# A float32 encoder trunk on one core: hidden tiles of two feed-forwards by seven block products in place of eight

## The chip, the core and the metric

The kernel runs on one core of one Trainium2 chip. The core's engines work side by side: TensorE (PE; its weight loads appear as PEld) multiplies into PSUM, which here is eight banks of 128x512 float32. VectorE (DVE), ScalarE (ACT) and GpSimd (POOL) work element by element, and SyncE (SP) issues most DMAs. Each engine runs its instructions in order. The metric is device time in microseconds from launch to end; lower is better.

## The reference, cut to what matters

One layer over 1024 prompt and 32 sample tokens, with D = 1024 features, 2816 hidden features and a modulation of nine rows computed from a condition vector c. All is float32.

```python
def swiglu(h, w1, w3, w2):
    return (jax.nn.silu(h @ w1) * (h @ w3)) @ w2

mod = (silu(c) @ w_ada + b_ada).reshape(B, 9, D)      # per group: prompt, sample
modulate(h, k) = h * (1 + mod[3k+1]) + mod[3k];  gate(k) = 1 + mod[3k+2]

x = layer_norm(x)
x = layer_norm(ALPHA*x + 0.5*gate(0) * swiglu(modulate(x, 0), ffn1_w1, ffn1_w3, ffn1_w2))
x = layer_norm(ALPHA*x + gate(1) * mixing(modulate(x, 1)))    # recurrent and gated branch
x = layer_norm(ALPHA*x + 0.5*gate(2) * swiglu(modulate(x, 2), ffn2_w1, ffn2_w3, ffn2_w2))
```

## The kernel before

**Layout.** Activations lie feature-major: features on the 128 partitions, eight feature tiles k, tokens along the free axis in three chunks of 384, 384 and 288 (the last ends with the 32 sample tokens). Products keep float32 precision by parts: each operand is split into a high part and a low part (type float32r), and a product is three passes over TensorE, high by high, high by low, low by high. `xh` and `xl` are the two parts of the modulated x, one tile for each chunk; `whl` holds the two parts of a weight tile. A split is a ScalarE copy (L177) for the high part and a subtraction (L178) on VectorE for the low part; while a norm follows a feed-forward, GpSimd does the subtraction.

**Feed-forward.** There are 22 hidden tiles of 128 features. `H(nf, t)` makes one: for w1, then w3, eight k-steps times three chunks times three passes, 144 matmuls, all through L132. ScalarE takes silu from PSUM (L659), VectorE multiplies by the w3 product (L666), and a split gives the two parts of `g`, the hidden tile. `F(nf, block)` multiplies the block's hidden tiles by w2 for eight output feature tiles m and three chunks; VectorE's `add_gated` (L713) multiplies each result by its gate and adds it into `xacc` (in the profile xa, and xb in the second feed-forward). A block is two hidden tiles, the last two blocks are [18] and [19, 20, 21]; F of a block comes one hidden tile after the block is complete.

**Weights.** 156 tiles of 128x1024 stream in the order of use: SP loads one into `raw` (four buffers), it is split into `whl` (five buffers), and `w_rel` goes on when a product has been issued.

**Beside the first feed-forward** `ada_rest` makes modulation rows 2 to 8, each in two halves of 512. VectorE adds up weight times condition in `acc` (L603), 16 instructions a half; TensorE sums over the partitions (psm); ScalarE copies the row out; GpSimd's queue issues a DMA to DRAM (`mrow`, L622) and two back (`mod`, L625). Such side programs are Python generators: `go` starts one and `poll`, called at each product, lets it write its next instructions when TensorE's program has advanced by as many us as it yielded. So the order on TensorE is that of the program; a scheduler orders the other engines' instructions.

Then come a layer norm, mixing, another norm, the second feed-forward with the same functions, and the last norm. The inner loop and the release of weights are

```python
for q in range(2):                                   # w1, w3
    w = self.w_get((f"f{nf}w{(1, 3)[q]}", t))
    ps = [self.ps() for _ in range(3)]
    for k in range(K):
        for c in range(3):
            self.h_mm(ps[c], w, c, k, k == 0, k == K - 1)
    self.w_rel()
```

Of the kernel before, what the change touches and what calls it, by code (L numbers as in the profile page):

```python
# [12 lines left out]
F32 = mybir.dt.float32  # L13
# [16 lines left out]
# token chunks; the last one ends with the 32 sample tokens  # L30
# [4 lines left out]
# columns of the packed per-feature vectors  # L35
# [37 lines left out]
def ffn_order():  # L73
    """Program of one feed-forward: ('H', t) and ('F', block), in order."""
    o = [("H", 0), ("H", 1)]
    nxt = 2
    for b in BLOCKS[:-1]:
        o.append(("H", nxt))
        nxt += 1
        o.append(("F", b))  # L80
        if len(b) == 2 and nxt < 19:
            o.append(("H", nxt))
            nxt += 1
    while nxt < FF:
        o.append(("H", nxt))
        nxt += 1
    o.append(("F", BLOCKS[-1]))
    return o


def stream_order():
    s = []
    for n in (1, 2):
        for kind, a in ffn_order():
            if kind == "H":
                s += [(f"f{n}w1", a), (f"f{n}w3", a)]
# [12 lines left out]

class Core:  # L110
    def __init__(self, tc, ins, outs):
        self.tc, self.nc = tc, tc.nc
        self.i, self.o = ins, outs
        self.pe = 0.0
        self.side = []
        self.ntot = 2
        self.mods = set()
        self.window = False
        self.ln_out = {}

# [14 lines left out]
    def go(self, gen, kind=None):  # L135
        """Run a side program beside the main one; it yields the time it has to wait."""
# [15 lines left out]
    def drain(self, e, out=False):  # L152
        """Finish a side program, or a norm up to its output; earlier norms first."""
# [7 lines left out]
    def w_init(self):  # L161
        self.order = stream_order()
        self.raws = {}
        self.ws = {}
        self.n_raw = self.n_split = self.n_rel = self.n_get = 0

    def w_raw(self):
        n = self.n_raw
        if n >= len(self.order):
            return  # L170
        r = self.wpool.tile([P, 1024], F32, tag="raw", name="raw", bufs=4)
        self.nc.sync.dma_start(r, self.i["wst"][n])
        self.raws[n] = r
# [5 lines left out]

    def w_split(self, e=None):  # L180
# [28 lines left out]
    def run(self):  # L209
# [4 lines left out]
        # pools over PSUM have eight one-bank buffers  # L214
# [38 lines left out]
        with tc.manual_schedule(engines={E.DVE, E.Activation, E.Pool}):  # L253
# [38 lines left out]
    def startup(self):  # L292
# [29 lines left out]
        # silu(c) in its two parts: [feature, k, (part, group)]  # L322
# [1028 lines left out]
```

## Time and profile before

| | us |
|---|---|
| median of three runs | 1987.72 |
| lowest and highest | 1986.25, 1989.53 |
| span of the profiled execution, first to last instruction | 1981.3 |
| the median less that span | 6.4 |
| TensorE busy | 1931.3 (97%) |
| VectorE busy | 1096.0 (55%) |
| ScalarE busy | 540.8 (27%) |
| GpSimd busy | 90.4 (5%) |

The span is the profiled execution's own time; what lies around it (launch and end) is in the runs alone. Busy shares are means over stages: start to 137 us, first feed-forward to 820 (the modulation's side program runs to 640), norm and mixing to 1211, second feed-forward to 1920, last norm to 1982. In a row of a timeline the first number is the start in us, the second the duration; "x12" counts instructions merged into the row, and square brackets give the idle time of that engine ahead of it and what ended it.

### The profile page before, as it was taken

The page shows a single profiled execution, that of the slowest core. Times are in us where ns is not written, and L with a number is a line of the kernel's source. Part 1 is how long each engine was busy: PE and PEld are TensorE (multiplying, and loading weights), DVE is VectorE, ACT ScalarE, POOL GpSimd, SP SyncE. Part 2 cuts the span into 40 slices and gives each one's busy share as a digit, 9 for nine tenths or more (in the row PEclk, how much of TensorE's full clock was granted, in tenths as well). Part 3 has the DMA queues.
Part 4 walks back from the last instruction along what each step waited for, and adds up shares of the span by engine and source line. Part 5 has one row for each costly group of instructions (what it writes and reads, how often), then busy time and mean ns, then how long its engine had stood idle before and what let it go on. Part 6 is the DMA issues. An engine that isn't in the chain of part 4 may idle for free.

```text
span 1981.3 us, 27961 instructions
## 1 busy us (share of the span) xinstructions
PE 1931.3 (97%) x11818; PEld 1886.5 (95%) x11818; DVE 1096.0 (55%) x1988; ACT 540.8 (27%) x848; POOL 90.4 (5%) x102
## 2 busy tenths in 40 slices
PE   7999999999999999989999999999999999999996
PEld 4899999999999999989889999999999999999996
DVE  8885765765664344763977375432442343244457
ACT  6542121212112111244544347111111111111114
POOL 2100000000000000022000000000000000000000
PEclk9999999999999999989899999999999999999998
DMA  7333223222322111121012311111111111110102
GB/s 281 130 126 101 95 84 117 97 75 96 102 95 71 54 43 44 54 80 67 14 59 67 130 36 40 54 43 54 43 34 63 43 43 44 54 43 33 33 1 88
DMA packets 40429, 140.13 MB, mean 71 GB/s; under 512 B 5588, under 2 KB 8276, under 8 KB 39536
## 3 DMA queue, kind: packets, MB, share of 16 engines
q1 hardware_dynamic: 37040, 128.98, 18.8%
q10 hardware_dynamic: 1920, 9.24, 1.2%
q0 software_dynamic: 1344, 0.12, 0.4%
q8 instruction: 93, 1.52, 0.3%
q14 instruction: 32, 0.26, 0.0%
HBM read 129.53 MB, written 8.79 MB: 70 GB/s over the span
## 4 chain that ended last, share of the span: by engine, by line
PE 78%; issue 10%; DVE 7%; ACT 2%; DMA 2%; POOL 0%; SPq 0%; POOLq 0%; DVEq 0%; ACTq 0%
PE ps L132 74%; PE psl L132 1%; DVE xl L462 1%; DVE acc L603 1%; PE psm L132 1%; PE psa L132 1%; DMA mod<-mrow 1%; PE psg L132 1%; DVE tot L719 0%; DMA mrow<-row 0%; ACT t L452 0%; DMA raw<-ada 0%; DVE xa L713 0%; DVE xb L832 0%; DVE t L843 0%
## 5 line engine op out<-in xcount | busy, mean ns | idle before, releaser
L132 PE MATMUL ps<-xh,whl 128*128 128x384 f32 (+1 forms) x5184 | 1245.4, 324 | 2.4 <-ACT xh L459 1.9
L132 PEld LDWEIGHTS ps<-xh,whl 128*128 128x128 f32 x5184 | 910.5, 189 | 7.0 <-ACT xh L459 2.1
L132 PE MATMUL ps<-xl,whl 128*128 128x384 f32 (+1 forms) x2592 | 839.3, 324 | 4.2 <-DVE xl L462 4.2
L132 PE MATMUL ps<-g,whl 128*128 128x384 f32 (+1 forms) x3168 | 522.2, 325 | 1.8 <-DVE xa L713 1.3
L132 PEld LDWEIGHTS ps<-g,whl 128*128 128x128 f32 x3168 | 513.2, 189 | 6.8 <-DVE xa L713 1.9
L132 PEld LDWEIGHTS ps<-xl,whl 128*128 128x128 f32 x2592 | 488.2, 188 | 7.7 <-DVE xl L462 6.0
L178 DVE TENSOR_TENSOR whl<-raw,whl 128x1024 fp32r<-128x1024 f32 x145 | 176.9, 1232 | 265.2 <-ACT whl L177 265.1
L177 ACT ACTIVATE whl<-raw 128x1024 fp32r<-128x1024 f32 x156 | 164.3, 1056 | 361.0 <-PE ps L132 356.6
L713 DVE SCALAR_TENSOR_TENSOR xb<-ps,gt,xb 128x384 f32<-128x384 f32 (+2 forms) x384 | 165.2, 486 | 109.6 <-PE ps L132 95.3
L666 DVE TENSOR_TENSOR s<-s,ps 128x384 f32<-128x384 f32 (+1 forms) x117 | 56.1, 520 | 246.9 <-PE ps L132 246.9
L603 DVE SCALAR_TENSOR_TENSOR acc<-raw,cs,acc 128x512 f32<-128x512 f32 x196 | 137.4, 747 | 56.9 <-DMA raw<-ada 56.9
L713 DVE SCALAR_TENSOR_TENSOR xa<-ps,gt,xa 128x256 f32<-128x256 f32 (+1 forms) x352 | 149.6, 487 | 17.1 <-PE ps L132 16.7
L177 ACT ACTIVATE g<-s 128x384 fp32r<-128x384 f32 x132 | 60.6, 488 | 342.7 <-DVE s L666 318.0
L659 ACT ACTIVATE s<-ps 128x384 f32<-128x384 f32 (+1 forms) x114 | 51.1, 457 | 277.2 <-PE ps L132 276.6
L178 DVE TENSOR_TENSOR g<-s,g 128x384 fp32r<-128x384 f32 x132 | 65.2, 519 | 3.8 <-ACT g L177 3.8
L476 POOL TENSOR_TENSOR r<-r,half 128x3 f32<-128x3 f32 x8 | 7.4, 920 | 1143.2 <-DVE r L475 1143.2
L462 DVE TENSOR_TENSOR xl<-t,xh 128x384 fp32r<-128x384 f32 (+3 forms) x48 | 42.4, 886 | 17.2 <-ACT xh L459 16.4
L132 PE MATMUL ps<-whl,xh 128*128 128x512 f32 (+1 forms) x144 | 46.4, 404 | 0.0
L177 ACT ACTIVATE acchl<-acc 128x512 fp32r<-128x512 f32 x28 | 17.7, 633 | 97.4 <-DVE acc L603 88.6
L452 ACT ACTIVATE t<-xa,AB 128x384 f32<-128x384 f32 (+1 forms) x64 | 34.1, 596 | 34.6 <-DVE AB L506 20.0
L132 PEld LDWEIGHTS ps<-whl,xh 128*128 128x128 f32 (+1 forms) x144 | 26.6, 187 | 7.1
L470 ACT ACTIVATE xb<-xb,aB,aG 128x384 f32<-128x384 f32 (+1 forms) x48 | 28.6, 669 | 14.3 <-DMA xb<-sp 14.3
(188 smaller groups left out, 899.8 us busy)
## 6 DMA issues: line engine op xcount, KB each, us to landing
raw<-wst SPq DMA_DIRECT2D x156, 512.0 KB, 3.2
raw<-ada SPq DMA_DIRECT2D x64, 512.0 KB, 3.3
wnat<-ada SPq DMA_DIRECT2D x4, 1024.0 KB, 13.0
xt<-x SPq DMA_DIRECT2D x7, 512.0 KB, 7.4
sp<-xa ACTq DMA_DIRECT2D x2, 1536.0 KB, 5.1
xb<-sp ACTq DMA_DIRECT2D x2, 1536.0 KB, 10.2
y<-xb SPq DMA_DIRECT2D x4, 768.0 KB, 3.2
sp<-xa ACTq DMA_DIRECT2D x1, 1152.0 KB, 4.1
```

Source lines behind the costliest of these rows:

```text
L132: self.nc.tensor.matmul(out, a, b, start=start, stop=stop, skip_group_check=True)
L177: self.nc.scalar.activation(dst_h, src, AF.Copy)
L178: (e or self.nc.vector).tensor_tensor(dst_l, src, dst_h.bitcast(F32), ALU.subtract)
L452: self.nc.scalar.activation(tmp[:, j, a:a + w], X[:, k, a:a + w], AF.Identity, scale=self.A[:, s, k, v:v + 1], bias=self.B[:, s, k, v:v + 1])
L462: V.tensor_tensor(xl, tmp, xh.bitcast(F32), ALU.subtract)
L470: return self.nc.scalar.activation(X[:, k, :], X[:, k, :], AF.Identity, scale=self.aG[:, s, k:k + 1], bias=self.aB[:, s, k:k + 1])
L476: self.nc.gpsimd.tensor_tensor(out, out, self.half[:n, :w], ALU.pow)
L603: V.scalar_tensor_tensor(acc[:, v, :], r[:, kk, :], self.cs[:, k, v:v + 1], acc[:, v, :], ALU.mult, ALU.add)
L659: self.nc.scalar.activation(s[:, :n], ps[c][:, :n], AF.Silu)
L666: self.nc.vector.tensor_tensor(s, s, ps[c][:, :n], ALU.mult)
L713: V.scalar_tensor_tensor(X[:, m, a + o:a + o + w], ps[:, o:o + w], self.gt[:, s, m, v:v + 1], X[:, m, a + o:a + o + w], ALU.mult, ALU.add)
```

## The change

For hidden tiles 9 to 21 of the first feed-forward and 3 to 21 of the second ("fast" tiles) the first two chunks are computed as a 2x2 block product in Winograd's form: the weights' blocks are (w1, w3) by the two halves of k, x's blocks are the two halves of k by chunks 0 and 1. Seven block products replace eight, over sums and differences of blocks: S1 to S4 of the weights, T1 to T4 of x. The third chunk stays an ordinary product (`third`).

- The weight sums are made in place in `raw` by GpSimd, four instructions of 128x512 a tile, and GpSimd also makes the low parts of S1 to S4. Weights are split in halves of 512 (`wh`, a ring of eight halves); `raw` has five buffers.
- The x sums are made once for each feed-forward (`combs`, `comb_last`): in the first, T1 and T3 on GpSimd, T2 and T4 on VectorE; in the second all on VectorE. T2 takes the place of chunk 1's first four feature tiles, so it is made after the last ordinary tile.
- Each fast tile has two ScalarE copies out of PSUM, four VectorE additions with PSUM and one without.
- Row blocks change: in the first feed-forward the first block has five tiles, then [5, 6], [7, 8] and pairs, in the second the first has three. F follows its block at once and goes in two halves of w2; its first two m are taken together over six banks, with chunk 1 last.
- `ada_rest` yields 2.9 us of TensorE's work after every two of its sums (before: 2.5 or 7.0 after four); `acc` has one buffer.

```diff
-BLOCKS = [[2 * b, 2 * b + 1] for b in range(9)] + [[18], [19, 20, 21]]
+BLOCKS = {1: [[0, 1, 2, 3, 4], [5, 6], [7, 8]] + [[b, b + 1] for b in range(9, 19, 2)] + [[19, 20, 21]],
+          2: [[0, 1, 2]] + [[b, b + 1] for b in range(3, 19, 2)] + [[19, 20, 21]]}
+FAST = {1: range(9, FF), 2: range(3, FF)}
+PARTS = ["A11", "A21", "A22", "S2", "A12", "S1", "S3", "S4"]
+RING, RAWS = 8, 5
...
+    def w_source(self, e):
...
+        if h == "A22":
+            G.tensor_tensor(a["A21"], a["A11"], a["A21"], ALU.subtract)      # S3
+        if h == "S2":
+            G.tensor_tensor(a["A22"], a["A22"], a["A21"], ALU.subtract)      # S2
+        if h == "S1":
+            G.tensor_tensor(a["A11"], a["A11"], a["A22"], ALU.add)           # S1
+        if h == "S4":
+            G.tensor_tensor(a["A12"], a["A12"], a["A22"], ALU.subtract)      # S4
...
-        e = e or (self.nc.gpsimd if self.window else None)
+        e = e or (self.nc.gpsimd if self.window or str(it[2])[0] == "S" else None)
...
+    def comb(self, dst, op, x, y, k, e):
+        t, u = self.new_s(), self.new_s()
+        for r, i in ((t, 0), (u, 1)):
+            e.tensor_tensor(r, x[i][:, k, :].bitcast(F32), y[i][:, k, :].bitcast(F32), op)
+        e.tensor_tensor(t, t, u, ALU.add)
+        self.split(dst[0][:, k, :], dst[1][:, k, :], t, e)
...
+    def H_fast(self, nf, t, later=False):        # w_rel calls left out
+        a11 = get("A11")
+        self.p_mm(pa, a11, B11, True, False)
+        S.activation(y0, pa[:, :n], AF.Copy)
+        third(0, 0, a11)
+        a21 = get("A21")
+        third(1, 0, a21)
+        self.p_mm(pb, get("S2"), self.T2, True, False)
+        add(y1, y0, pb)
+        a12 = get("A12")
+        self.p_mm(pa, a12, B21, False, True)
+        z0 = self.silu(0, pa)
+        third(0, 1, a12)
+        y2 = self.silu(2, sides[0])
+        self.p_mm(pc, get("S1"), self.T1, True, False)
+        S.activation(z1, pc[:, :n], AF.Copy)
+        self.p_mm(pb, get("S3"), self.T3, False, True)
+        add(y0, y0, pb)
+        V.tensor_tensor(z1, z1, y0, ALU.add)
+        a22 = get("A22")
+        self.p_mm(pf, a22, self.T4, True, True)
+        add(y0, y0, pf)
+        self.glu_end(g, 0, z0, y0)
+        third(1, 1, a22)
+        self.glu_end(g, 2, y2, sides[1][:, :CH[2][1]])
+        self.p_mm(pc, get("S4"), B22, False, True)
+        add(y1, y1, pc)
+        S.activation(y1, y1, AF.Silu)
+        self.glu_end(g, 1, y1, z1)
...
     def F(self, nf, block):
-        for m in range(K):
-            ps = [self.ps() for _ in range(3)]
-            for j in range(len(block)):
-                for c in range(3):
-                    self.f_mm(ps[c], ws[j], gs[j], PIECES[c], m, j == 0, j == len(block) - 1)
+        for h in range(2):
+            for ms in ((0, 1), (2,), (3,)) if h == 0 else ((0,), (1,), (2,), (3,)):
+                for j in range(J):
+                    for m, c in ([(m, c) for c in (0, 2, 1) for m in ms] if j == J - 1 else
+                                 [(m, c) for m in ms for c in range(3)]):
+                        self.f_mm(ps[m][c], ws[j], gs[j], PIECES[c], 4 * h + m, j == 0, j == J - 1)
```

`p_mm` is a block product, four k-steps of three passes; `add(out, x, ps)` is one VectorE addition with PSUM; `glu_end` is the multiplication and the split.

**TensorE in the second feed-forward.** Before, one k-step of a hidden tile: `xh_85` to `xh_87` are the high parts of chunks 0 to 2, `xl_88` to `xl_90` the low parts.

```order
L132 MATMUL ps<-xh_85,whl 128x384
L132 MATMUL ps<-xl_88,whl 128x384
L132 MATMUL ps<-xh_85,whl 128x384
L132 MATMUL ps<-xh_86,whl 128x384
L132 MATMUL ps<-xl_89,whl 128x384
L132 MATMUL ps<-xh_86,whl 128x384
L132 MATMUL ps<-xh_87,whl 128x288
L132 MATMUL ps<-xl_90,whl 128x288
L132 MATMUL ps<-xh_87,whl 128x288
```

Now, in the middle of a fast tile: the end of a product of the third chunk, S1 by T1 and S3 by T3 (`tx`), then the start of A22 by T4 (`T_11889` and `T_11890` are its two parts).

```order
L152 MATMUL ps<-xl_90,wh 128x288
L152 MATMUL ps<-xh_87,wh 128x288
L152 MATMUL ps<-tx,wh 128x384 x24
L152 MATMUL ps<-T_11889,wh 128x384
L152 MATMUL ps<-T_11890,wh 128x384
L152 MATMUL ps<-T_11889,wh 128x384 x2
L152 MATMUL ps<-T_11890,wh 128x384
```

Chunks 0 and 1 no longer come at each k-step; they are taken up in runs of twelve matmuls, each run with a weight block of its own.

**GpSimd in the second feed-forward.** Before, from mixing to the end of the program it has only the steps of the norms' roots.

```order
L476 TENSOR_TENSOR vrs<-vrs,half 128x1 x7
L1121 MEMSET xab 128x3
L1122 MEMSET xab 128x2
L476 TENSOR_TENSOR vrs<-vrs,half 128x1
L476 TENSOR_TENSOR vrs<-vrs,half 32x1
L476 TENSOR_TENSOR r<-r,half 128x3 x5
```

Now, for each fast tile, the four sums in `raw` and four low parts in `wh`.

```order
L239 TENSOR_TENSOR raw<-raw 128x512
L241 TENSOR_TENSOR raw<-raw 128x512
L243 TENSOR_TENSOR raw<-raw 128x512
L210 TENSOR_TENSOR wh<-raw,wh 128x512 x2
L245 TENSOR_TENSOR raw<-raw 128x512
```

**ScalarE there**, now, in one fast tile: copies of products (L874, L897), silus (L669, L916) and the high parts of weights (L209).

```order
L209 ACTIVATE wh<-raw 128x512 x4
L874 ACTIVATE s<-ps 128x384
L209 ACTIVATE wh<-raw 128x512 x3
L669 ACTIVATE s<-ps 128x384
L669 ACTIVATE s<-ps 128x288
L209 ACTIVATE wh<-raw 128x512
L897 ACTIVATE s<-ps 128x384
L209 ACTIVATE wh<-raw 128x512 x2
```

The high parts of S1 to S4 stand among the silus and copies of the tile before, and each needs GpSimd's sum.

**VectorE beside the modulation.** Before, F's evictions (L713) alternate with the modulation's sums (L603).

```order
L713 SCALAR_TENSOR_TENSOR xa_108<-ps,gt,xa_108 128x32
L627 TENSOR_TENSOR mod<-mod,vec 128x8
L603 SCALAR_TENSOR_TENSOR acc<-raw,cs,acc 128x512 x2
L713 SCALAR_TENSOR_TENSOR xa_106<-ps,gt,xa_106 128x384
L713 SCALAR_TENSOR_TENSOR xa_107<-ps,gt,xa_107 128x384
L713 SCALAR_TENSOR_TENSOR xa_108<-ps,gt,xa_108 128x256
L713 SCALAR_TENSOR_TENSOR xa_108<-ps,gt,xa_108 128x32
L603 SCALAR_TENSOR_TENSOR acc<-raw,cs,acc 128x512
```

Now, in a fast tile, the modulation's sums (L759, L761) alternate with the block sums (L867, L902), multiplications (L674) and low parts (L210).

```order
L210 TENSOR_TENSOR wh<-raw,wh 128x512
L759 TENSOR_SCALAR acc<-araw,cs 128x512 x2
L867 TENSOR_TENSOR s<-s,ps 128x384
L761 SCALAR_TENSOR_TENSOR acc<-araw,cs,acc 128x512
L902 TENSOR_TENSOR s<-s 128x384
L761 SCALAR_TENSOR_TENSOR acc<-araw,cs,acc 128x512
L867 TENSOR_TENSOR s<-s,ps 128x384
L761 SCALAR_TENSOR_TENSOR acc<-araw,cs,acc 128x512
L674 TENSOR_TENSOR s<-s 128x384
L674 TENSOR_TENSOR s<-s,ps 128x288
```

Where a fast tile is made, every block sum now stands one modulation sum behind the product that it evicts.

More of the change, by code (lines that the diff above doesn't have):

```diff
@@ L180, in w_split @@
     def w_split(self, e=None):
         n = self.n_split
-        e = e or (self.nc.gpsimd if self.window else None)
         if n >= len(self.order):
             return
-        while self.n_raw <= n:
+        it = self.order[n]
+        e = e or (self.nc.gpsimd if self.window or str(it[2])[0] == "S" else None)
+        while not all(r in self.raws for r in raws_of(it)):
             self.w_raw()
-        w = self.wpool.tile([P, 2, 1024], F32R, tag="whl", name="whl", bufs=5)
-        r = self.raws.pop(n)
@@ L189, in w_split @@
-        self.split(w[:, 0, :], w[:, 1, :], r, e)
-        self.ws[n] = w
+        w = self.w_tile(it)
+        self.split(w[:, 0, :], w[:, 1, :], self.w_source(it), e)
+        self.ws[it] = w
         self.n_split += 1
     def w_get(self, what):
-        n = self.n_get
-        assert self.order[n] == what, (self.order[n], what)
-        while self.n_split <= n:
+        if len(what) == 2:
+            return [self.w_get((*what, h)) for h in range(2)]
+        while what not in self.ws:
             self.w_split()
-        self.n_get += 1
@@ new lines, in ada_rest, with sums, out @@
+        rows, pre = {}, None
+        def sums(v, acc, ps):
+            hl = [self.apool.tile([P, 512], F32R, tag="tot", name="acchl", bufs=self.ntot) for _ in range(2)]
+            self.split(hl[0], hl[1], acc[:, v, :])
+            yield
+            yield
+            for q in range(2):
+                self.mm(ps[0:2, :], self.one_r[:, v, :], hl[q], v + q == 0, v + q == 2)
+        def out(m, h, ps):
+            d = rows[m, h] = self.dram.tile([2, 512], F32, name=f"mrow{m}_{h}")
+            row = self.apool.tile([P, 512], F32, tag="tot", name="row", bufs=self.ntot)[0:2, :]
+            nc.scalar.activation(row, ps[0:2, :], AF.Copy)
+            nc.gpsimd.dma_start(d, row)
@@ L663, in H, with g_tag @@
[L663 to L667 removed]
+                ss = [self.silu(c, ps[c]) for c in range(3)]
+        g = self.gs[t] = self.new_g(self.g_tag(nf, t))
+        for c in range(3):
+            self.glu_end(g, c, ss[c], ps[c][:, :CH[c][1]])
+    def g_tag(self, nf, t):
+        return "t4" if t == 2 else "tx" if t == LAST[2] or t in BLOCKS[nf][0][3:] else "g"
@@ new lines, in p_mm, with block @@
+    def p_mm(self, ps, w, x, first, last):
+        xh, xl = x
+        n = xh.shape[2]
+        for k in range(4):
+            wh, wl = w[:, 0, k * P:(k + 1) * P], w[:, 1, k * P:(k + 1) * P]
+            self.mm(ps[:, :n], wh, xh[:, k, :], first and k == 0, False)
+            self.mm(ps[:, :n], wh, xl[:, k, :], False, False)
+            self.mm(ps[:, :n], wl, xh[:, k, :], False, last and k == 3)
+            self.poll()
+    def block(self, i, c):
+        return self.xh[c][:, 4 * i:4 * i + 4, :], self.xl[c][:, 4 * i:4 * i + 4, :]
@@ L767, in ffn @@
+    def ffn(self, nf, combs, bg=None):
+        before = [b for b in BLOCKS[nf] if b[0] not in FAST[nf]]
+        if nf == 2:
+            combs = combs()
+        for b in BLOCKS[nf][:-1]:
+            for t in b:
+                if t in self.gs and self.gs[t] is not None:
+                    continue
+                if t in FAST[nf]:
+                    self.H_fast(nf, t)
+                else:
+                    self.H(nf, t)
+            if b == BLOCKS[nf][0]:
                 while nf == 1 and 2 not in self.mods:
@@ L791, in last_f @@
+        third = self.H_fast(nf, block[-1], True)
+        self.open.add((f"f{nf}w2", True))
+        ws = [[self.w_get((f"f{nf}w2", t, h)) for t in block] for h in range(2)]
         gs = [self.gs.pop(t) for t in block]
-        hidden(1)
         lns, prev = [], None
```

477 lines of the change are left out of this document (304 added, 173 removed).

## Prediction, made before the changed kernel ran

> **What bounds the kernel now.** I read the page's first lines, then busy time by stretch, then the groups by line and shape, and last the timeline where an idle gap or a slowed row showed. The page: span, TensorE's row, its granted clock in 40 slices, and the chain of work that ended last, by engine.
>
> ```profile
> span 1981.3 us, 27961 instructions
> PE 1931.3 (97%) x11818; PEld 1886.5 (95%) x11818; DVE 1096.0 (55%) x1988; ACT 540.8 (27%) x848; POOL 90.4 (5%) x102
> PEclk9999999999999999989899999999999999999998
> PE 78%; issue 10%; DVE 7%; ACT 2%; DMA 2%; POOL 0%; SPq 0%; POOLq 0%; DVEq 0%; ACTq 0%
> ```
>
> TensorE is busy for 97% at nearly full clock, and the chain that ended last is mostly TensorE. Busy time by stretch follows (columns: stretch, length, busy time of PE, PE loads, VectorE, ScalarE and GpSimd, then granted clock, DMA share, GB/s). The rows are the start, the first feed-forward beside the modulation, its rest, mixing, the second feed-forward and the end. The last row is a piece of the second feed-forward alone.
>
> ```profile
> 60.00:137.00 77.00, 74.04 (x480) 71.30 (x480) 60.97 (x111) 41.50 (x74) 9.09 (x8) 0.98 0.41 134
> 137.00:640.00 503.00, 502.11 (x3092) 494.92 (x3093) 316.82 (x588) 98.67 (x162) 25.03 (x37) 1.00 0.29 94
> 640.00:820.00 180.00, 180.00 (x1099) 178.72 (x1098) 83.87 (x178) 28.09 (x43) 0.59 (x1) 1.00 0.12 39
> 820.00:1211.00 391.00, 378.73 (x2213) 361.83 (x2213) 258.56 (x394) 188.89 (x272) 35.09 (x32) 0.97 0.18 65
> 1211.00:1920.00 709.00, 709.00 (x4398) 708.02 (x4398) 279.05 (x527) 125.33 (x213) 0.00 (x0) 1.00 0.13 43
> 1920.00:1982.00 62.00, 44.01 (x261) 40.63 (x259) 46.28 (x79) 23.15 (x34) 1.93 (x2) 0.86 0.19 70
> 1215.00:1500.00 285.00, 285.00 (x1788) 285.00 (x1787) 111.27 (x207) 57.85 (x100) 0.00 (x0) 1.00 0.15 51
> ```
>
> From 137 to 820 us and from 1211 to 1920 us TensorE does not idle (0.9 us in 1392), at clock 1.00. A matmul removed there shortens the span by its pitch, if the other engines still keep up. VectorE stands at 39% in the second feed-forward (111.27 of 285) and at 63% beside the modulation (316.82 of 503); GpSimd does nothing in the one and issues small DMAs in the other. DMA engines are busy for 29% at most, and the same 156 weight tiles are still loaded, so transfers are not the bound.
>
> **The removed products.** The pitch of a matmul is the distance of two starts in a run of hidden-tile products, three matmuls to a group.
>
> ```profile
> 1196.23 0.33 PE L132 MATMUL ps<-xl,whl 128*128 128x384 f32 x1
> 1204.03 0.33 PE L132 MATMUL ps<-xl,whl 128*128 128x384 f32 x1
> 817.95 0.29 PE L132 MATMUL ps<-xl,whl 128*128 128x288 f32 x1
> 821.95 0.30 PE L132 MATMUL ps<-xl,whl 128*128 128x288 f32 x1
> ```
>
> Between the first two lie 15 groups of three: 7.80/45 = 0.1733 us for 384 columns. Between the last two lie 10 groups: 4.00/30 = 0.1333 us for 288. A product of two chunks with both w1 and w3 was 2x8x2 = 32 k-steps of three matmuls. Seven block products of four k-steps are 28. So each fast tile loses 4x3 = 12 matmuls of 0.1733 us, 2.08 us. 13 tiles in the first and 19 in the second feed-forward: 32 x 2.08 = **-66.6 us** (-27.0 and -39.5). The third chunk's 48 matmuls stay.
>
> **What the other engines get.** Groups by line and shape, with busy time, mean ns of one, and idle before by releaser:
>
> ```profile
> L178 DVE TENSOR_TENSOR whl<-raw,whl 128x1024 fp32r<-128x1024 f32 x145 | 176.9, 1232 | 265.2 <-ACT whl L177 265.1
> L177 ACT ACTIVATE whl<-raw 128x1024 fp32r<-128x1024 f32 x156 | 164.3, 1056 | 361.0 <-PE ps L132 356.6 <-PE psa L132 4.4
> L178 POOL TENSOR_TENSOR whl<-raw,whl 128x1024 fp32r<-128x1024 f32 x11 | 28.5, 2602 | 67.1 <-ACT whl L177 67.1
> L178 DVE TENSOR_TENSOR acchl<-acc,acchl 128x512 fp32r<-128x512 f32 x28 | 19.1, 690 | 3.1 <-ACT acchl L177 2.3
> L177 ACT ACTIVATE acchl<-acc 128x512 fp32r<-128x512 f32 x28 | 17.7, 633 | 97.4 <-DVE acc L603 88.6 <-DVE whl L178 5.6 <-issue 3.0
> L603 DVE SCALAR_TENSOR_TENSOR acc<-raw,cs,acc 128x512 f32<-128x512 f32 x196 | 137.4, 747 | 56.9 <-DMA raw<-ada 56.9
> L713 DVE SCALAR_TENSOR_TENSOR xa<-ps,gt,xa 128x384 f32<-128x384 f32 x176 | 101.3, 613 | 17.1 <-PE ps L132 16.7
> L713 DVE SCALAR_TENSOR_TENSOR xa<-ps,gt,xa 128x256 f32<-128x256 f32 x88 | 42.0, 477 | 0.0
> L713 DVE SCALAR_TENSOR_TENSOR xa<-ps,gt,xa 128x32 f32<-128x32 f32 x88 | 21.5, 244 | 0.0
> L178 DVE TENSOR_TENSOR g<-s,g 128x384 fp32r<-128x384 f32 x88 | 48.6, 553 | 3.8 <-ACT g L177 3.8
> L177 ACT ACTIVATE g<-s 128x384 fp32r<-128x384 f32 x88 | 45.4, 517 | 342.0 <-DVE s L666 318.0 <-DVE s L572 24.0
> L666 DVE TENSOR_TENSOR s<-s,ps 128x384 f32<-128x384 f32 x78 | 41.6, 554 | 246.9 <-PE ps L132 246.9
> ```
>
> The unit is a two-tile block: two fast tiles of 84x0.1733+48x0.1333 = 21.0 us and F's 8x2 products of 1.44 us, 65.0 us of TensorE. In it VectorE evicts F (16x0.613+8x(0.477+0.244) = 15.6), makes the low parts of 12 weight halves (12x0.69 = 8.3), adds ten block sums (10x0.554 = 5.5), and makes four mults and four low parts of 384 columns with two of 288 each (3.1+3.1): 35.6 us. The old block by the same means was 15.6+6x1.232+6.2 = 29.2 of 69.1 us, 42%, where the stretch shows 39%, so means overstate by some 7%: I take 33 us. GpSimd gets 8 combinations and 8 low parts of 512 columns at half of 2602: 16x1.30 = 20.8 us, which was zero. ScalarE, at 20% (57.85 of 285), gets 20 half splits of 0.63 in place of 6 whole ones of 1.06, and four copies of 0.52: +8 us, about a third of 65.
>
> In the **second feed-forward** VectorE's 33 and GpSimd's 20.8 us do not fill 65 even when one excludes the other. Weights are split eight halves ahead, 15 us or more of TensorE's work. I cost the combinations at nothing there; if that cover went, a fast tile would wait for GpSimd.
>
> Beside the **modulation** it is tight. From the order of the instructions, 14 halves of 16 sums go on one for each 31.5 us of TensorE, and fast tiles run beside the last 190 us of it, 2.9 blocks. A half is 16x0.747+2x0.69 = 13.3 us on VectorE, 2.06 in a block: 27.4. VectorE: 35.6+27.4 = 63, less 7%: 59 of 65 us. GpSimd's 20.8 stand beside that, and they are not independent: beside a GpSimd subtraction a VectorE one of two SBUF operands takes several times its time, while an eviction from PSUM runs on.
>
> ```profile
> 35.46 2.41 POOL L403 TENSOR_TENSOR g<-raw,g 128x1024 fp32r<-128x1024 f32 x1 [3.24 <-ACT g L397]
> 35.48 2.71 DVE L462 TENSOR_TENSOR xl<-t,xh 128x288 fp32r<-128x288 f32 x1
> 61.95 0.46 DVE L462 TENSOR_TENSOR xl<-t,xh 128x288 fp32r<-128x288 f32 x1
> 847.28 9.46 POOL L178 TENSOR_TENSOR whl<-raw,whl 128x1024 fp32r<-128x1024 f32 x3 [18.25 <-ACT whl L177]
> 851.40 0.63 DVE L713 SCALAR_TENSOR_TENSOR xa<-ps,gt,xa 128x32 f32<-128x32 f32 x2
> ```
>
> The same operation took 2.71 us beside GpSimd's 2.41 and 0.46 alone; an eviction at 851.40 took its usual time. So a block needs between 59 us (all of GpSimd's work lands on evictions and adds from PSUM, some 22 us of the 59) and 80 (none does), against 65.0: a loss of 0 to 15 a block, 0 to 43 in 2.9 blocks. GpSimd also carries the modulation's DMAs, and waits there:
>
> ```profile
> POOL mod L625 <- DMA mrow<-row: 45.7, 14, 4.0
> 164.22 0.54 POOL L622 DMA_DIRECT2D mrow<-row  x1 [36.28 <-ACT row L620]
> 167.01 1.51 POOL L625 DMA_DIRECT2D mod<-mrow  x2 [2.25 <-DMA mrow<-row]
> ```
>
> 0.54+3.3+1.51 is some 5.3 us a half in which combinations queue behind; the 15 us of lead hide one such wait. I take a third of the way between the bounds, since evictions interleave with the sums: **+14** (0 to 43).
>
> The Trainium skill, page "SBUF — State Buffer", section "Who interferes with whom", says that VectorE with two SBUF operands and GpSimd take a port pair in turn, each for a whole instruction, and the loser stands still. The 2.71 beside 2.41 us agrees; by that rule alone the block is nearer its upper bound than I put it, which is the second case below.
>
> The **x combinations** T1 to T4, 16 k-steps of three adds and a low part each, with the high part on ScalarE: in the first feed-forward two of them are on GpSimd during the first blocks, two on VectorE, 8x4x0.553 = 17.7 us in one block before the first fast tile. In the second all four are on VectorE, 35 us over three blocks. VectorE's free 40% takes them; the last, T4, is made right behind a block and is due in the next tile: bounds 0 and 10, nearer 0 since the tile's first product that needs it is the sixth. **+3** and **+1**.
>
> **F's start.** A fast tile's last product releases a chain (add 0.55, silu about as long as ScalarE's 0.52, mult 0.55, high 0.52, low 0.55 = 2.7 us) to chunk 1's g, which F's second tile needs. F now takes two m together, chunk 1 last, which leaves 2x1.44 for the first tile and 2x(0.52+0.40) for the second's chunks 0 and 2, 4.7 us. I take 13 starts at 0.2: **+2.6** (0 to 20, at 1.5 each).
>
> **The front.** Block 1's wait on VectorE's evictions beside the modulation goes, as its F now comes three tiles later.
>
> ```profile
> 137.89 2.29 PE L132 MATMUL ps<-g,whl 128*128 128x288 f32 x13 [1.31 <-DVE xa L713]
> 1929.66 0.80 PE L132 MATMUL psl<-ones,t 128*128 128x1 f32 x6 [1.48 <-DVE t L848]
> 1930.32 3.89 PE L132 MATMUL ps<-g,whl 128*128 128x384 f32 x12
> ```
>
> Bounds: 0 and the 3.0 us of idle between 60 and 137 us; I take the 1.3 shown and a little: **-1.5**. Three F blocks fewer (two and one) save VectorE 3x15.6 us of evictions, on no path.
>
> **Sum**: -66.6+14+3+1+2.6-1.5 = -47.5. Against the profiled span 1981.3 that is 1933.8. The runs' median, 1987.7, lies 6.4 us above that span; that stays, and the forecast is **1940 us**, 2.4% less.
>
> **Rivals.** (a) The whole gain comes out: the loss beside the modulation, combinations and F's starts are all hidden. VectorE's 59 of 65 speaks for it, the exclusion against: 1987.7-66.6-1.5 = 1920, 1918 to 1926 with the small terms. (b) Exclusion binds: GpSimd's 20.8 us come on top of VectorE's 59 in each of 2.9 blocks, +43, for 1920+43+6.6 = 1969. For it: the rows at 35 us. Against: evictions run on. (c) Slower: ScalarE works in order, and the high parts of S2 and S4 wait for GpSimd's combinations ahead of the silus. If GpSimd falls behind, TensorE waits in every fast tile, and it pays twice, since after an idle gap its matmuls run slow: above, 1.48 us of idle are followed by 12 matmuls in 3.89 us, 0.31 each against 0.173, 1.65 us more. 3.1 us in 32 tiles are 100: 2020 us. It decides at 66.6/32 = 2.1 us a tile. Against it: at 137.89 a gap of 1.31 left the pace as it was (13 matmuls in 2.29), and the lead of 15 us.
>
> The Trainium skill, page "TensorE: Matmul & The Clock Gate", section "Why this matters", would have gaps stay free below about 3 us, by which (c) could not start from gaps so short and would be struck out. The rows at 1929.66 show otherwise here, so it keeps its chance.
>
> **How the numbers follow.** Forecast (1926 to 1958): 0.50. (a): 0.22. (b), 1958 to 1983: 0.18. (c): 0.07. No net change, by losses that just eat 66.6 us: 0.03. Within 0.2%, 4 us, a run cannot be told from no change. So faster 0.90, same 0.03, slower 0.07. The range goes from 1914 (all gains at their upper bounds, 1918, less the runs' scatter of 3) to 1976, which leaves out the upper edge of (b) and all of (c).
>
> **What the profile after would show.** Right: 384 matmuls of 384 columns fewer, TensorE without idle and at clock 1.00 in the second feed-forward, which is some 39 us shorter; VectorE there near 50%, GpSimd near 32%. Idle of TensorE between some 340 and 530 us, 10 to 20 us, released by VectorE's evictions or ScalarE's wh parts. Wrong: idle of TensorE in the second feed-forward behind GpSimd's combinations, or its granted clock below 0.98 there; or none at all beside the modulation, which would be (a).

## The result, and the profile after

The changed kernel takes 1943.4 us (median of four runs, 1938.7 to 1945.3) against 1987.0 before: ratio 0.9776, 95% interval 0.9761 to 0.9792, some 44 us or 2.2% less. 1940 was forecast, in a range of 1914 to 1976. The page after, first lines and chain:

```profile
span 1942.7 us, 28443 instructions
PE 1870.9 (96%) x11434; PEld 1820.6 (94%) x11434; DVE 1291.3 (66%) x2296; ACT 696.4 (36%) x1228; POOL 483.2 (25%) x398
PEclk9999999999998999989989999999999999999998
PE 81%; DVE 10%; ACT 3%; issue 2%; DMA 2%; POOL 2%; SPq 0%; POOLq 0%; DVEq 0%; ACTq 0%
```

TensorE has 11818-11434 = 384 matmuls fewer, as counted. The profiled execution took 1944.4 us by the clock of the runs, 1.7 above its span; the span fell by 38.6, the median by 43.6, because the profiled execution of before was one of the quickest (1981.3+1.7 = 1983.0).

Busy time by stretch, after; columns as in the prediction. First the first feed-forward in three pieces (before the fast tiles; VectorE's x sums at 357 to 406 us and the fast tiles beside the modulation, whose last sum stands at 588 us; fast tiles alone), then the second:

```profile
80.00:340.00 260.00, 256.13 (x1549) 250.43 (x1550) 172.99 (x298) 76.29 (x146) 54.52 (x53) 0.99 0.33 107
340.00:640.00 300.00, 282.15 (x1685) 273.16 (x1684) 255.65 (x451) 87.90 (x166) 105.84 (x86) 0.97 0.26 84
640.00:790.00 150.00, 150.00 (x944) 150.00 (x943) 81.58 (x150) 47.86 (x91) 55.45 (x41) 1.00 0.15 50
1170.00:1880.00 710.00, 710.00 (x4443) 709.31 (x4442) 422.78 (x768) 248.24 (x460) 211.18 (x154) 1.00 0.14 45
```

The same two first pieces before:

```profile
80.00:340.00 260.00, 258.21 (x1586) 253.44 (x1585) 177.45 (x314) 69.48 (x118) 14.56 (x21) 1.00 0.34 112
340.00:640.00 300.00, 300.00 (x1849) 295.70 (x1849) 186.00 (x349) 58.62 (x97) 14.79 (x22) 1.00 0.28 90
```

From 640 us on, fast tiles cost TensorE no idle time and no clock: 710 of 710 us busy at 1.00 in the second feed-forward, with VectorE at 60% (422.78) and GpSimd at 30% (211.18). From 340 to 640 us, where fast tiles and modulation meet, TensorE idles 17.9 us and its clock is 0.97; before, neither. What ended its idle times between 137 and 850 us:

```profile
PE ps L152 <- DVE s L674: 7.1, 4, 3.0
PE ps L152 <- ACT s L874: 5.0, 2, 3.5
PE ps L152 <- ACT g L209: 4.7, 4, 1.8
PE ps L152 <- DVE s L867: 2.1, 1, 2.1
PE ps L152 <- DVE g L210: 1.4, 4, 0.5
```

No row waits for a weight tile `wh`. TensorE waits for VectorE's block sums and multiplications (L867, L674), for ScalarE's copies of products (L874), and for parts of g. One such wait, from the timelines of GpSimd, VectorE, ScalarE and TensorE in turn:

```profile
426.85 1.27 POOL L210 TENSOR_TENSOR wh<-raw,wh 128x512 fp32r<-128x512 f32 x1
...
426.32 2.36 DVE L761 SCALAR_TENSOR_TENSOR acc<-araw,cs,acc 128x512 f32<-128x512 f32 x1
428.61 0.55 DVE L674 TENSOR_TENSOR s<-s 128x384 f32<-128x384 f32 x1
...
429.19 0.52 ACT L209 ACTIVATE g<-s 128x384 fp32r<-128x384 f32 x1 [2.23 <-DVE s L674]
429.62 0.47 ACT L874 ACTIVATE s<-ps 128x384 f32<-128x384 f32 x1
...
430.14 0.44 PE L152 MATMUL ps<-xh,wh 128*128 128x384 f32 x1 [3.47 <-ACT s L874]
```

One of the modulation's sums takes 2.36 us beside GpSimd's low part, where the group's mean before was 747 ns. The multiplication (L674) of the tile before stands behind it, ScalarE's part of g waits 2.23 us for that, and its copy of y0 (L874), which frees the bank into which A12 by B21 goes on, stands behind that part. TensorE idles 3.47 us. Behind this gap its clock is still 1.00; behind two others, which end at 371.6 us (3.01 us long) and at 588.3 us (2.07 us), it falls to about a half (columns as above):

```profile
430.00:440.00 10.00, 9.86 (x59) 9.86 (x60) 8.93 (x15) 5.12 (x11) 0.24 (x1) 1.00 0.63 219
370.00:377.00 7.00, 5.42 (x19) 5.14 (x20) 5.91 (x11) 0.86 (x2) 0.38 (x1) 0.52 0.22 75
588.00:602.00 14.00, 10.70 (x33) 9.39 (x34) 11.27 (x19) 3.48 (x7) 4.51 (x3) 0.53 0.11 39
```

To compare kernels I use the delay of TensorE: the start of a matmul in the trace less the pitches of all matmuls ahead of it. The pitch is columns/2.4 ns plus 13.3 ns, the straight line through the prediction's 0.1733 us for 384 columns and 0.1333 us for 288; for the small matmuls at the start it is too long, so only the difference of the two columns counts. The delay grew as follows:

| growth of the delay, us | before | after |
|---|---|---|
| start to 80 us | -4.1 | -1.7 |
| 80 to 360 | 4.9 | 10.4 |
| 360 to 640 (x sums, then fast tiles beside the modulation) | 2.3 | 29.9 |
| 640 to 800 (fast tiles alone) | 1.9 | 0.1 |
| 800 to 1040 (norm, mixing) | 24.6 | 21.7 |
| 1040 to the last norm (second feed-forward) | -0.7 | -3.9 |

Against before, 27.6 us were lost in one place and 7.9 ahead of it, and 7.9 came back behind 640 us; 66.6 less 27.6 is the span's 38.6 within half a us. The part from 360 to 640 us differs between executions: 29.9 here, 30.0 and 31.5 in ff1_fast and acchl_dve below, 37.1 in front_gp, whose edits lie elsewhere or make no difference there. So a difference of less than some 7 us in this stretch between two traces says little.

### The profile page after: what moved, and what is told of

It is laid out like the page before. It is cut to its first block, busy times and chain, and to the rows that moved or that the text cites. A ratio compares the mean times of both kernels' runs of the same rounds, so it can differ in the third digit from the quotient of the medians.

```text
span 1942.7 us, 28443 instructions
## 1 busy us (share of the span) xinstructions
PE 1870.9 (96%) x11434; PEld 1820.6 (94%) x11434; DVE 1291.3 (66%) x2296; ACT 696.4 (36%) x1228; POOL 483.2 (25%) x398
## 3 DMA queue, kind: packets, MB, share of 16 engines
q10 hardware_dynamic: 1920, 9.24, 1.2%
## 4 chain that ended last, share of the span: by engine, by line
PE 81%; DVE 10%; ACT 3%; issue 2%; DMA 2%; POOL 2%; SPq 0%; POOLq 0%; DVEq 0%; ACTq 0%
PE ps L152 78%; DVE acc L761 1%; PE psl L152 1%; DVE xl L548 1%; DVE wh L210 1%; DMA mod<-mrow 1%; PE psa L152 1%; PE psz L152 1%; PE psm L152 1%; DMA araw<-ada 1%; DVE s L674 0%; PE psg L152 0%; ACT t L538 0%; POOL s L818 0%; DVE tot L980 0%
## 5 line engine op out<-in xcount | busy, mean ns | idle before, releaser
L152 PE MATMUL ps<-xh,wh 128*128 128x384 f32 (+1 forms) x4016 | 953.7, 320 | 6.9 <-ACT s L874 5.0
L152 PEld LDWEIGHTS ps<-xh,wh 128*128 128x128 f32 x4016 | 698.9, 189 | 12.2 <-ACT s L874 5.7
L152 PE MATMUL ps<-xl,wh 128*128 128x384 f32 (+1 forms) x2008 | 641.7, 320 | 3.3 <-DVE xl L548 3.2
L152 PE MATMUL ps<-g,wh 128*128 128x384 f32 (+1 forms) x2808 | 474.8, 328 | 17.0 <-DVE s L674 7.1
L152 PEld LDWEIGHTS ps<-g,wh 128*128 128x128 f32 x2808 | 461.3, 191 | 26.8 <-DVE s L674 8.4
L209 ACT ACTIVATE wh<-raw 128x512 fp32r<-128x512 f32 x428 | 266.2, 628 | 524.9 <-PE ps L152 436.8
L152 PEld LDWEIGHTS ps<-xl,wh 128*128 128x128 f32 x2008 | 378.6, 189 | 7.1 <-DVE xl L548 5.3
L210 DVE TENSOR_TENSOR wh<-raw,wh 128x512 fp32r<-128x512 f32 x283 | 204.6, 729 | 246.0 <-ACT wh L209 244.6
L210 POOL TENSOR_TENSOR wh<-raw,wh 128x512 fp32r<-128x512 f32 x145 | 208.8, 1442 | 321.8 <-ACT wh L209 321.5
L761 DVE SCALAR_TENSOR_TENSOR acc<-araw,cs,acc 128x512 f32<-128x512 f32 x196 | 154.1, 825 | 15.3 <-DMA araw<-ada 15.1
L209 ACT ACTIVATE g<-s 128x384 fp32r<-128x384 f32 (+1 forms) x126 | 60.7, 492 | 138.7 <-DVE s L674 138.7
L210 DVE TENSOR_TENSOR g<-s,g 128x384 fp32r<-128x384 f32 (+1 forms) x126 | 84.9, 683 | 23.6 <-ACT g L209 22.5
L867 DVE TENSOR_TENSOR s<-s,ps 128x384 f32<-128x384 f32 x128 | 70.5, 551 | 37.4 <-PE ps L152 37.3
L669 ACT ACTIVATE s<-ps 128x384 f32<-128x384 f32 (+1 forms) x100 | 44.9, 452 | 99.4 <-PE ps L152 99.1
```

The lines of the kernel that those rows point to most:

```text
L152: self.nc.tensor.matmul(out, a, b, start=start, stop=stop, skip_group_check=True)
L209: self.nc.scalar.activation(dst_h, src, AF.Copy)
L210: (e or self.nc.vector).tensor_tensor(dst_l, src, dst_h.bitcast(F32), ALU.subtract)
L669: self.nc.scalar.activation(s, x[:, :n], AF.Silu)
L761: V.scalar_tensor_tensor(acc[:, v, :], r[:, kk, :], self.cs[:, k, v:v + 1], acc[:, v, :], ALU.mult, ALU.add)
L867: V.tensor_tensor(out, x, ps[:, :n], ALU.add)
```

## The experiments

Theory Q put the loss down to VectorE's queue, in which block sums stand behind the modulation's sums; theory L to GpSimd's instructions, which hold up VectorE's; theory W to weights that come late behind GpSimd's sums; theory H, later, to ScalarE's own queue.

**ff2_fast**: the first feed-forward's fast tiles are only the last three.

```diff
-FAST = {1: range(9, FF), 2: range(3, FF)}
+FAST = {1: range(19, FF), 2: range(3, FF)}
```

> Tiles 9 to 18 of the first feed-forward go back to eight products: 10 x 2.08 = 20.8 us more TensorE work than the changed kernel (1943.4). Theory Q (VectorE's queue: block sums and parts of g stand behind the modulation's sums): the first feed-forward's loss of some 30 us shrinks to 5 to 10 with the fast tiles gone from beside the modulation, so 1939 to 1946, about the changed kernel's time. Rival (the loss comes from the new row blocks, the halves of weights or the front, not from fast tiles): the loss stays, 1964.

1946.4 us (ratio to before 0.9794, 0.9779 to 0.9808). Ten fast tiles less, 20.8 us more work, and 3 us of time.

```profile
340.00:640.00 300.00, 297.11 (x1826) 291.70 (x1825) 189.17 (x394) 64.68 (x122) 17.41 (x25) 1.00 0.29 93
```

With the same new blocks and halves of weights, TensorE idles 2.9 us here in place of 17.9. So the loss belongs to the fast tiles with the x sums made for them. What idle time is left is almost all at one place:

```profile
587.26 1.00 PE L152 MATMUL ps<-g,wh 128*128 128x288 f32 x4 [2.32 <-DVE s L674]
```

The multiplication (L674) stands there in VectorE's queue behind a chain of small instructions (`spt`, a softplus for mixing) that follow the modulation's last row.

**mod_thin**: the modulation's accumulating sums over 64 columns.

```diff
-V.scalar_tensor_tensor(acc[:, v, :], r[:, kk, :], self.cs[:, k, v:v + 1], acc[:, v, :], ...)
+V.scalar_tensor_tensor(acc[:, v, :64], r[:, kk, :64], self.cs[:, k, v:v + 1], acc[:, v, :64], ...)
```

> Each of the modulation's 196 accumulating sums (L761) works on 64 of its 512 columns; the rest is left out. Theory Q: without these 150 us of VectorE the first feed-forward loses 5 us at most, so 1943 - 27 = 1916 (1911 to 1922). Theory L (GpSimd's combinations and low parts hold up VectorE's operations of two SBUF operands): low parts and products of g are still held up, and about half the loss stays: 1930. Theory W (weights come late by GpSimd's sums): no gain, 1943.

1921.2 us (0.9669, 0.9653 to 0.9685): 22 us less than the changed kernel.

```profile
340.00:640.00 300.00, 291.21 (x1780) 284.62 (x1779) 211.38 (x458) 94.26 (x180) 105.43 (x88) 0.99 0.27 88
```

VectorE is down from 256 to 211 us of 300, GpSimd as before at 105. The delay grows by 14.9 here in place of 29.9. That is against W, which had GpSimd's work as the cause by itself; it fits Q, a little short of its 1916.

**no_gp**: GpSimd out of the first feed-forward's fast tiles.

```diff
+        if nm == "f1":                        # in w_source: no sums of blocks
+            return a[{"S1": "A11", "S2": "A22", "S3": "A21", "S4": "A12"}.get(h, h)]
...
+        if it[0] == "f1" and it[2][0] == "S":  # in w_split: both parts by ScalarE
+            src = self.w_source(it)
+            for i in range(2):
+                self.nc.scalar.activation(w[:, i, :], src, AF.Copy)
```

> In the first feed-forward GpSimd's sums of weight blocks are left out, and the low parts of S1 to S4 are plain ScalarE copies (the products are of the blocks themselves), so GpSimd is out of the fast tiles there; VectorE's instructions stay as they are. Theory Q: the modulation's sums still stand ahead of block sums; only their stretch (825 ns in place of 747, and g's low parts) goes, so a loss of 20 stays: 1935 (1930 to 1940). Theory L: nearly all of the loss goes, 1917 (1913 to 1923). Theory W: as L.

1922.0 us (0.9669, 0.9651 to 0.9687). The stretch, and in the second fence the modulation's sums in it (mean ns after the comma):

```profile
340.00:640.00 300.00, 294.04 (x1802) 287.49 (x1801) 226.13 (x468) 113.94 (x216) 16.93 (x24) 0.99 0.28 90
```

```profile
L768 DVE SCALAR_TENSOR_TENSOR acc<-araw,cs,acc 128x512 f32<-128x512 f32 x90 | 64.5, 745 | 5.1 <-DMA araw<-ada 5.1
```

In the changed kernel the same group:

```profile
L761 DVE SCALAR_TENSOR_TENSOR acc<-araw,cs,acc 128x512 f32<-128x512 f32 x92 | 77.9, 873 | 7.9 <-DMA araw<-ada 7.8
```

With GpSimd gone the sums are back at 745 ns, and the delay from 360 to 640 us grows by 11.4, 7.8 of it by 400 us, where VectorE makes T2 and T4; there TensorE waits for the multiplication (here L681):

```profile
368.78 5.41 PE L152 MATMUL ps<-g,wh 128*128 128x288 f32 x18 [2.00 <-DVE s L681]
```

Q alone had expected a loss of 20 to stay; it fell. Either of the two, the sums or GpSimd, can be taken away, and most of the loss goes. What was open is whether GpSimd's instructions themselves or the wait for their results did it.

**gp_dummy**: no_gp, with eight GpSimd subtractions a tile on which no product waits.

```diff
+            for i in range(2):
+                self.nc.gpsimd.tensor_tensor(src, src, w[:, 0, :].bitcast(F32), ALU.subtract)
```

> As no_gp (S1 to S4 are the plain blocks, their low parts ScalarE copies), but for each of the four parts GpSimd makes two subtractions of 128x512 in place in the raw block, after ScalarE has read it: eight operations a tile as in the changed kernel, and no product waits for them. Theory L (GpSimd's instructions hold up VectorE's): the loss comes back, 1943 (1936 to 1948), and the modulation's sums take 850 ns or more again. Theory W (weights came late behind GpSimd's sums): 1922 as no_gp.

1942.6 us (0.9774, 0.9755 to 0.9793): all of the loss is back.

```profile
340.00:640.00 300.00, 280.78 (x1682) 272.69 (x1681) 255.90 (x451) 104.27 (x201) 105.67 (x86) 0.97 0.26 83
```

```profile
L770 DVE SCALAR_TENSOR_TENSOR acc<-araw,cs,acc 128x512 f32<-128x512 f32 x90 | 79.3, 908 | 6.3 <-DMA araw<-ada 6.3
```

```profile
PE ps L152 <- DVE s L876: 8.1, 3, 4.4
```

The last line is TensorE's longest wait between 340 and 640 us, in total 8.1 us, for block sums (L876 here); in no_gp it does not wait for them.

L is shown and W is out: instructions of GpSimd that no product waits for (only the reuse of buffers does) stretch VectorE's sums from 745 to 908 ns and cost 20.5 us.

**front_gp**: the low part of the second weight half at the start on GpSimd.

```diff
-        for h in range(2):
-            self.w_split()
+        self.w_split()
+        self.w_split(nc.gpsimd)
```

> At the start the low part of the second half of the first weight tile is made by GpSimd in place of VectorE, where it stands ahead of the modulation's first row (L514). Expected: the idle of 1.86 us at 29 us and the half clock behind it go, 3 us: 1940 (1938 to 1942). Rival: the row still waits for the first half's low part, which itself waits for a ring buffer, so 1943.

1945.2 us (0.9786, 0.9769 to 0.9803): no gain. Of TensorE's timeline, the changed kernel's wait at 30 us, then the waits with the edit:

```profile
30.93 0.25 PE L584 MATMUL psa<-idn,arow 2*128 2x2 f32 x2 [1.86 <-DVE arow L514]
```

```profile
30.40 0.28 PE L584 MATMUL psa<-idn,arow 2*128 2x2 f32 x2 [0.51 <-DVE arow L514]
...
40.63 0.44 PE L152 MATMUL ps<-xl,wh 128*128 128x384 f32 x1 [1.16 <-DVE xl L548]
```

The idle went, and most of it came back 10 us later.

**mod_paced** and **mod_slow**: fewer sums beside a fast block.

```diff
-            w = 2.9
+            w = 2.5 if not self.fast_on else 4.5    # mod_paced; fast_on from the last ordinary block's F
+            w = 3.5                                 # mod_slow
```

> The modulation's side program yields 2.5 us of TensorE's work up to the last ordinary block and 4.5 beside the fast tiles (2.9 throughout in the changed kernel). Beside a fast block stand 19 us of sums in place of 27: VectorE 51, GpSimd 21, against 65. Theory L+Q (too much of both at once): the loss of 28 us there falls to 8 to 15, 1928 (1922 to 1935). Rival (each sum costs TensorE the same wherever it stands): 1943; or VectorE before the fast tiles, at 67%, becomes the bound and gives it back: 1943.

> The modulation's side program yields 3.5 us throughout in place of 2.9, so it ends near 700 us in place of 600, with 23 us of sums in a fast block in place of 27. Theory L+Q: loss of 28 falls to about 18, but over one more block: 1936 (1930 to 1942). Rival, each sum costs the same: 1943.

1956.2 (0.9844, 0.9829 to 0.9858) and 1951.3 (0.9822, 0.9805 to 0.9838): both slower than the changed kernel. Both expectations missed. Of mod_paced, a wait at the pace of 2.5, and busy time:

```profile
273.21 0.59 PE L152 MATMUL psm<-acchl,one_r 128*2 128x512 f32 x1 [8.76 <-ACT acchl L209]
```

```profile
340.00:640.00 300.00, 284.19 (x1677) 275.82 (x1676) 229.84 (x390) 87.17 (x163) 98.99 (x79) 0.95 0.24 78
640.00:790.00 150.00, 144.85 (x897) 144.53 (x897) 86.19 (x179) 43.21 (x82) 51.75 (x39) 0.98 0.15 50
```

Of mod_slow, the rest of the first feed-forward, and its sums between 340 and 640 us:

```profile
640.00:790.00 150.00, 141.72 (x857) 138.51 (x856) 99.74 (x200) 45.41 (x85) 55.30 (x44) 0.97 0.21 68
```

```profile
L761 DVE SCALAR_TENSOR_TENSOR acc<-araw,cs,acc 128x512 f32<-128x512 f32 x94 | 89.3, 982 | 2.3 <-DMA araw<-ada 2.2
```

From 360 to 640 us the delay grows by 31 in both, as in the changed kernel, although mod_paced's VectorE is busy for 77% and not 85%. So VectorE's busy time alone does not tell the loss. A sum now takes 982 ns in mod_slow and 962 in mod_paced, where it was 873; why single sums should suffer more is not shown. Behind 640 us another 8 and 13 us are lost. mod_slow's sums go on to 692 us, mod_paced's end at 600. Most of this loss stands beside the `spt` chain, which runs at 723 to 738 us in mod_slow and at 641 to 654 us in mod_paced (in the changed kernel at 617 to 628 us, where it costs little); in mod_paced it is one wait:

```profile
657.22 0.69 PE L152 MATMUL ps<-xh,wh 128*128 128x384 f32 x1 [5.15 <-ACT s L875]
```

The wait at 273 us is a further loss at the pace of 2.5: the high part of the sums (acchl) stands on ScalarE behind those of T1 and T3, which wait for GpSimd.

**acchl_dve**: that high part made by VectorE.

```diff
-            self.split(hl[0], hl[1], acc[:, v, :])
+            V.tensor_copy(hl[0], acc[:, v, :])
+            V.tensor_tensor(hl[1], acc[:, v, :], hl[0].bitcast(F32), ALU.subtract)
```

> The high part of the modulation's sums (28 copies of 128x512) is made by VectorE in place of ScalarE. Theory H (ScalarE, in order, waits for the sums at that copy, up to 9 us, with copies of y0 and parts of g behind it): the loss falls by half or more, 1925 to 1934. Theory L+Q (VectorE and GpSimd have too much together): VectorE gets 28 x 0.5 = 14 us more, some 6 of it beside fast tiles, so no gain: 1943 to 1950.

1943.8 us (0.9794, 0.9777 to 0.9810), and the delay from 360 to 640 us grows by 31.5: H falls.

**ff1_fast**: the second feed-forward's fast tiles are only the last three (FAST[2] = range(19, FF)).

> Tiles 3 to 18 of the second feed-forward go back to eight products, those of the first stay by seven: 16 x 2.08 = 33.3 us more work than the changed kernel. If the second feed-forward keeps all of its gain (no idle there), 1977 (1974 to 1980). Rival (combinations or F's start cost some there): less than 33, 1965 to 1973.

1981.6 us (0.9981, 0.9969 to 0.9992), 38 more than the changed kernel. Sixteen fast tiles of the second feed-forward are worth their 33.3 us and 5 more, which lies outside the expected range; 1.9 us of the 5 are idle time of TensorE at 1824 to 1828 us, where the x sums are now made, and the rest stays open. The other side of it: all fast tiles of the first and three of the second, 33.3 us of products, gain 0.2%, about 4 us.

**fast13** and **fast15**: fast tiles of the first feed-forward from 13 or 15 on, meant to leave two blocks or one beside the modulation.

```diff
-FAST = {1: range(9, FF), 2: range(3, FF)}
+FAST = {1: range(13, FF), 2: range(3, FF)}    # fast13
+FAST = {1: range(15, FF), 2: range(3, FF)}    # fast15
```

> Fast tiles start at 13: 12.5 us less TensorE work than ff2_fast (1946), two fast blocks beside the sums. Theory L+Q, with some 9 us lost in each block beside the sums against 4.2 gained: 1946 - 12.5 + 18 = 1951, or 1943 if the last of them is half clear. Rival (the loss comes at the first fast tiles, by the x combinations, not by each block): 1934 plus at most 5.

> Fast tiles of the first feed-forward start at 15 in place of 9: 6 x 2.08 = 12.5 us more TensorE work than the changed kernel, 8.3 less than ff2_fast (1946). Theory L+Q: one fast block, 15 and 16, still stands beside the modulation's sums and loses some 8 us, the later ones lose nothing: 1938 to 1944. If all of it loses nothing: 1938. Rival (every fast block of this feed-forward loses, with the sums or without): 1946.

1935.8 (0.9754, 0.9740 to 0.9769) and 1932.8 (0.9741, 0.9725 to 0.9758). In the stretch from 340 to 640 us, of fast13 and then of fast15:

```profile
340.00:640.00 300.00, 291.39 (x1776) 283.93 (x1775) 227.57 (x437) 78.92 (x150) 62.38 (x56) 0.99 0.26 87
```

```profile
340.00:640.00 300.00, 297.68 (x1828) 292.11 (x1827) 215.85 (x430) 74.11 (x140) 38.95 (x40) 0.99 0.27 89
```

The delay grows by 14.8 and 6.5. The modulation's sums end at 570 and 550 us here (588 in the changed kernel, with three blocks beside them). So in fast13 one fast block, 13 and 14, stands beside them, and in fast15 none. The sums show it, in fast13 and then in fast15:

```profile
L761 DVE SCALAR_TENSOR_TENSOR acc<-araw,cs,acc 128x512 f32<-128x512 f32 x90 | 72.4, 848 | 0.6 <-DMA araw<-ada 0.6
L761 DVE SCALAR_TENSOR_TENSOR acc<-araw,cs,acc 128x512 f32<-128x512 f32 x92 | 64.3, 745 | 4.3 <-DMA araw<-ada 4.3
```

A fast block beside the modulation thus costs 7.5 to 8 us (14.8 less 6.5 for one, 29.9 less 14.8 for the changed kernel's two more) and gains 4.2; one that stands behind it costs next to nothing. Of fast15's 6.5 us, 4.5 come at 580 to 590 us, and ff2_fast, without a fast tile or x sums there, loses 3.9 at the same place to the `spt` chain. Both runs came out better than Theory L+Q expected, since fewer blocks stood beside the sums than it counted. fast13's time lies in its rival's range, but not for the rival's reason: two further blocks beside the sums cost 15.1 us more.

**fast15_front**, both edits together:

> fast15 (1932.8) with front_gp's edit, the low part of the second half of the first weight tile on GpSimd: the idle of 1.86 us ahead of the modulation's second transposed row goes to 0.5. If that stays a gain, and the half clock behind it goes with it, 1930 (1929 to 1932); if it is given back to a later wait at the start, as in front_gp, 1933.

1933.4 us (0.9739, 0.9726 to 0.9752): no different from fast15. fast15 beats the changed kernel by 10 us with fewer fast tiles, and the intervals of their ratios to before (up to 0.9758, from 0.9761) lie apart.

## Why the prediction was right, point by point

- **Removed products**, -66.6: held. 384 matmuls are gone. The second feed-forward's tiles have their full worth: ff1_fast gives 38 us for sixteen of them, 33.3 by the sum.
- **Beside the modulation**, +14 of 0 to 43: the right mechanism, sized too small. From 360 to 640 us the delay grew by 27.6 more than before (29.9 less 2.3). Of that, 6.7 lie by 400 us, with the x sums; the other 21 lie beside the fast tiles, and gp_dummy against no_gp puts 19 on the exclusion (30.3 less 11.4). I had placed the loss a third of the way between the bounds; it is near the middle. The bounds were of busy time, and the rows at 426 us show a loss of latency: a block sum or multiplication that stands behind one stretched modulation sum is late, and ScalarE and TensorE pass it on. mod_paced, with VectorE at 77%, loses as much, which fits; that all of the loss is of this kind is argued. Behind some of the gaps the clock is at 0.52, which the term had left out.
- **x combinations**, +3 and +1. Between 360 and 400 us, where T2 and T4 are made, the delay grows by 7.0 in the changed kernel and by 7.8 in no_gp, against 0.3 before and 1.0 in ff2_fast, which makes them later: the term was too small, inside its bounds of 0 to 10. In the second feed-forward it is 0.
- **F's start**, +2.6: in the second feed-forward 0 (no idle in 710 us). In the first it can't be told from the exclusion; in no_gp, where that is gone, TensorE idles some 1.5 us in F of three fast blocks.
- **The front**, -1.5: wrong in sign. TensorE is 2.4 us later at 80 us and another 5.5 at 360. VectorE makes two weight halves ahead of the modulation's row, which waits (1.86 us). The wait at 137 us went, but the later F of the longer first block meets the same modulation's sums: TensorE waits for L674 twice, 1.7 us each, at 182 and 292 us. In mod_slow, with the sums spread more thinly, the delay from 80 to 360 us grows by 4.5 in place of 10.4.
- **Weights** at nothing: held; no row of TensorE waits for `wh`.
- **The signs**: TensorE without idle and at clock 1.00 in the second feed-forward, as told; GpSimd there at 30% for 32%. VectorE is at 60%, not near 50%: the share left out the x sums, and with GpSimd beside it VectorE's multiplication of two SBUF operands took 768 ns (554 were counted) and g's low part 634 (553). It cost nothing there. Idle time beside the modulation came to 17.9 us, as told (10 to 20), but it went on to 596 us, and no part of it was released by `wh`.
- **The sum**: 19.1 us of losses were forecast, 27.6 show in the trace. Not foreseen were 7.9 us less delay behind 640 us (1.8 to 800, 2.9 to 1040, 3.2 in the second feed-forward; their cause stays open), which cover the front's 7.9 by chance. That 1940 came within 4 us of the median is partly luck: the profiled execution of before lay 4 us under its median, so the forecast took 6.4 us for the time around the span, which is 1.7. By the spans 47.5 us were forecast and 38.6 came.

Of the rivals, (a) did not come: 1920 is what no_gp and mod_thin reach, each with part of the work left out. (b) was nearest by its mechanism, with some 20 us in place of 43. (c) stayed out: a gap of over 2.1 us in every fast tile did not occur. Of the gaps that did occur, some were followed by a lower clock, as it supposed (3.01 us ahead of 371.6), and others not (3.47 us ahead of 430.1).

## What to carry to other kernels

Where TensorE is the bound and another engine pair is to take work off it, put the work where the two have slack together. VectorE and GpSimd hold each other up, so add their shares: at 60% and 30% the second feed-forward gave all of its 39.5 us; at 85% and 35% the first gave next to nothing. Such a pair can cost latency though neither is full, so look at the single long row in the timeline and at what stands behind it in its queue. When a stage has a busy and a quiet half, start in the quiet one, as fast15 does: ten microseconds more, with less of the change.

## What the runs showed of the hardware

GpSimd's subtractions of 128x512 on SBUF stretched VectorE's sums of two SBUF operands from 745 to 908 ns on average (no_gp and gp_dummy), a single one to 2.36 us in the changed kernel, though in gp_dummy no product waited for GpSimd. VectorE's additions with one operand in PSUM kept their time: 551 ns, where the multiplication with PSUM took 554 before. The Trainium skill, page "SBUF — State Buffer", section "Who interferes with whom", says that a VectorE instruction with two SBUF inputs contends with a GpSimd instruction that reads SBUF, and one with at most one SBUF input, outside the two-port modes, does not; the trace agrees with both. GpSimd is held up in turn. Its low part of 512 columns took 1442 ns on average:

```profile
L867 DVE TENSOR_TENSOR s<-s,ps 128x384 f32<-128x384 f32 x128 | 70.5, 551 | 37.4 <-PE ps L152 37.3
L210 POOL TENSOR_TENSOR wh<-raw,wh 128x512 fp32r<-128x512 f32 x145 | 208.8, 1442 | 321.8 <-ACT wh L209 321.5
```

Of these 145, the 44 beside which VectorE ran no instruction of two SBUF operands took 1263 to 1299 ns, the others 1508 on average and up to 3213. The estimate's 1301, half of 2602 for 1024 columns, was right for the undisturbed ones alone.

Gaps of TensorE of 3.01 us at 368 and 2.07 us at 586 were followed by 7 and 14 us at a clock of 0.52 and 0.53; in these 300 us that comes to some 9 us (0.03 of the stretch) beside 17.9 of idle. The length of a gap does not decide it alone: 1.71 us at 292 us was followed by 3.4 us at half clock, while 1.71 at 182 us and 3.47 at 427 us left the clock at 1.00.
